# State-space outputs, decay gates and chunk products of neighbouring tiles in turn on groups of the array's columns and rows, with an arena of 64 slots

## The chip, the cores and the metric

One core of a Trainium2 chip runs the whole program. The metric is the device time of one execution in microseconds (us). Before the change three runs gave 1535.45, 1535.64 and 1537.04 us, the median 1535.64.

## What is computed

The reference passes 256 tokens of width 1024 through two blocks, in float32. The first block has two layers with attention, pooling and a gated linear attention (GLA). The second block has one layer: an RWKV recurrence and a state-space branch (S5) whose results are merged, and then a feed-forward part with a short convolution. Three places matter here.

The decay gates of the GLA, for both directions, from 16 columns each of the projected input:

```python
log_a_f = (jax.nn.log_sigmoid((zz['gla_af'] @ af_w2 + af_b).astype(f32)) / GLA_TAU)
log_a_b = (jax.nn.log_sigmoid((zz['gla_ab'] @ ab_w2 + ab_b).astype(f32)) / GLA_TAU)
```

The state-space branch: 32 groups of 64 complex states, run over the tokens, and read out by a complex matrix of which the real part counts:

```python
_, states = lax.associative_scan(s5_combine, (a_elems, bu), axis=1)
y = jnp.real(jnp.einsum('gcp,blgp->blgc', c, states)) + d * ug
y = jax.nn.gelu(y.reshape(bsz, L, S5_WIDTH))
```

The RWKV recurrence over the tokens, eight heads of 64, of which the kernel makes four chunks of 64 tokens:

```python
sa = jnp.einsum('bhij,bhj->bhi', S, a_t)
S = S * w_t[:, :, None, :] + sa[..., None] * b_t[:, :, None, :] + v_t[..., None] * k_t[:, :, None, :]
```

## The kernel before

All activations lie transposed, 128 features by 256 tokens (512 where context and sequence lie side by side). Weights come from one large array in units, by DMAs that SyncE (SP) issues (`unit`); `split` cuts each into a rounded high part `wh` (ScalarE, line 425) and a rest `wl` (VectorE or GpSimd, line 427), with four buffers of each, and `mm3` (line 442) multiplies with three products. Seven buffers hold raw weights.

Working tiles of 128x512 come from the `Arena`: NSLOT slots, a queue of free ones; `get` takes the oldest free slot and `put` hands one back at the end. Whoever writes a slot waits for its former readers. PSUM has four buffers for large products (`pmm`) and two each in the pools `pa` and `pb`.

The order of the work is made in two steps. The code of a branch is written as a generator, and `weave` runs two of them in turn by counts written by hand, a chain of dependent steps and a filler with independent products. The Tile framework then lays out each engine's instructions from that order, by priority and readiness, and sets the waits.

What the change touches:

`gla_decay` (line 1025), at the head of the GLA chain of each layer. For each of four heads it multiplies 32 rows (64 to 95) of the tile `misc` by 32 rows of `gw` into a PSUM tile `pgate` of 512 columns (line 1030), and VectorE adds a bias and makes the input of the logarithm (lines 1032 to 1034). Later, per level of the GLA, VectorE writes a fresh arena tile `E` at lines 1136 and 1137, out of two tiles that no matmul writes.

`s5_chain` (line 1543): sixteen tiles. For each, SP loads a table, PE makes `bu` (line 1587; two tiles at a time, in two groups of 32 rows), VectorE and GpSimd turn it (1590 to 1593), and a step later `recur` runs the recurrence on VectorE (scan at line 1559, products at 1560 and 1561, the last on GpSimd). Two steps later `output` (line 1564) makes the real output: four float32 products of 128 rows, 32 columns and 256 tokens, added up in one quarter (32 partitions) of a PSUM tile `py5`, which the traces call `py`. The quarter is i % 4. After each fourth tile VectorE (1575) and ScalarE take the sum. `py` is also the name of the attention's output (line 886), where products for two heads go in turn to two groups of 64 columns, and `pmod` (line 609) is filled by four products in turn in four groups of 32 columns.

```python
for n, (w_, x_) in enumerate(((cre, t1[:, 0:256]), (cren, t1[:, 256:512]), (cimn, t2[:, 0:256]),
                              (cimn, t2[:, 256:512]))):
    nc.tensor.matmul(pys[-1][rows, C], w_[:, cc_], x_, start=n == 0, stop=n == 3)
```

`rwkv_chain` (line 1643): products of 64 rows by 64 columns, each in one quarter of the array, which its operands' partitions and its output's partitions choose. Per head the scores `sc` (line 1771) and `scl` (1773), with `cp` (token half, output rows) outside and source inside; VectorE masks `sc` at 1776. Then inverses by doubling (`pQ`, `pY`, `pX`, lines 1800 to 1808), `pw` (1827, eight heads of one half and then eight of the other), and the loop over four chunks: `prh` (1846, four products for even heads, VectorE's sum, four for odd heads), `pu` (1853), the new state `pmn` (1861, 1862, per head k and then b), the output `pyo` (1868, 1869, likewise) and `pyi` (1878). `bonus_of` (line 1682), `head_bcast` (`hb`, line 1668, from a copy at 1665) and `nk` (1657) belong to its preparation.

A float32 matmul of the program runs as two records in the trace, two passes with a weight load each.

The chain and the branch are woven by these lines at the end of `second_block`: the columns of the RWKV part with seven steps of the state-space chain, then fourteen steps of the RWKV chain with five, ten with the rest, and what is left with `merge1`.

Of the kernel before, what the change touches and what calls it, by code (L numbers as in the profile page):

```python
# [27 lines left out]
FF = 2816  # L28
MLA_SCALE = 96 ** -0.5
TAU = 16.0  # L30
NSLOT = 62
MOD_AT = (0, 1, 4)
S5_EARLY = (7, 5)


# [44 lines left out]
def _pad_rows(a, at, rows=P):  # L80
    out = np.zeros((rows, a.shape[1]), a.dtype)
    out[at:at + a.shape[0]] = a
    return out
# [88 lines left out]
def _win_cols(w, name, t):  # L172
    if name == "misc":
        kr = w[:, OFF["kr"]:OFF["kr"] + 32]
        z = np.zeros((D, 32), w.dtype)
        return np.concatenate([kr, kr[:, ROPE_PERM], w[:, OFF["af"]:OFF["af"] + 32], z], 1)
    o = OFF[name] + P * t
    return w[:, o:o + P]

# [111 lines left out]
def gate_weights(inp, l):  # L291

    gw = np.zeros((32, 4, 2, 64), np.float32)
    gw[:16, :, 0] = np.asarray(inp["gla_af_w2"][l]).reshape(16, 4, 64)
    gw[16:, :, 1] = np.asarray(inp["gla_ab_w2"][l]).reshape(16, 4, 64)
    return _pad_rows(gw.reshape(32, 512), 64)

# [375 lines left out]
def trunk(b, l, xs, st, A):  # L675
# [349 lines left out]

    def gla_decay():
        es = []
        for hd in range(4):
            ps = b.pa.tile([P, 512], F32, tag="p", name="pgate")
            nc.tensor.matmul(ps, gw[64:96, hd * P:(hd + 1) * P], misc[64:96], start=True, stop=True)  # L1030
            e, a = S.get(), S.get()
            nc.vector.tensor_scalar(a, ps, v("gb", hd), None, ALU.add)
            nc.vector.scalar_tensor_tensor(e, a, -1.0, a, ALU.mult, ALU.min)
            nc.vector.tensor_scalar(a, a, 0.0, None, ALU.min)
            nc.scalar.activation(e, e, AF.Exp)
            es.append(e)
            la.append(a)
        one = b.after(es, 1.0)
        for e in es:
            nc.scalar.activation(e, e, AF.Ln, bias=one)  # L1040
        for e, a in zip(es, la):
            nc.vector.tensor_sub(a, a, e)
            S.put(e)
        S.put(misc, gw)
# [423 lines left out]
def second_block(b, xs, st, A):  # L1468
# [74 lines left out]
    def s5_chain():  # L1543
# [17 lines left out]
            nc.gpsimd.tensor_tensor(h2(t2), h2(g5), h2(tab)[:, ::-1], ALU.mult)  # L1561
            S.put(g5, tab)

        def output(i):
            _, t1, t2 = parts[i]
            rows, cc_ = slice(32 * (i % 4), 32 * (i % 4) + 32), slice(32 * i, 32 * i + 32)
            if i % 4 == 0:
                pys.append(b.pb.tile([P, 512], F32, tag="p", name="py5"))
            for n, (w_, x_) in enumerate(((cre, t1[:, 0:256]), (cren, t1[:, 256:512]), (cimn, t2[:, 0:256]),
                                          (cimn, t2[:, 256:512]))):  # L1570
                nc.tensor.matmul(pys[-1][rows, C], w_[:, cc_], x_, start=n == 0, stop=n == 3)
            S.put(t1, t2)
            if i % 4 == 3:
                u_ = us[i // 4]
                nc.vector.scalar_tensor_tensor(u_.ap, u_.ap, v("d", i // 4), pys[-1][:, C], ALU.mult, ALU.add)
                nc.scalar.activation(u_.ap, u_.ap, AF.Gelu_apprx_tanh)

        for i in range(16):
            tab = S.get()
            nc.sync.dma_start(tab, b.s5["tab"][i])  # L1580
# [13 lines left out]
            parts.append((tab, t1, t2))  # L1594
            if i:
                recur(i - 1)
            if i > 1:
                output(i - 2)
            yield
        recur(15)  # L1600
        output(14)
        output(15)
        S.put(*s5w, sbr, sbi)
        wg = b.unit(("glu",))
        ysp = []
# [35 lines left out]
    def rwkv_chain():  # L1641
# [116 lines left out]
        for bt in range(2):  # L1758
            Lm, Y, X_ = S.get(), S.get(), S.get()
            for hd in range(4 * bt, 4 * bt + 4):  # L1760
# [3 lines left out]
                pl_ = b.pa.tile([P, 512], F32, tag="p", name="scl")  # L1764
                ar3 = AR[q].rearrange("p (a t) -> p a t", a=2)
                for cc in range(2):
                    for cp in range(2):
                        t0 = cc * P + cp * CH
                        orow = slice(cp * CH, cp * CH + CH)
                        for n, src in enumerate((BT, KT)):  # L1770
                            nc.tensor.matmul(ps[orow, cc * 256 + n * P:cc * 256 + n * P + P].rearrange("p (a t) -> p a t", a=2),
                                             src[q].ap[rows, t0:t0 + CH], ar3[rows, :, t0:t0 + CH], start=True, stop=True)
                        nc.tensor.matmul(pl_[orow, cc * CH:cc * CH + CH], AR[q][rows, t0:t0 + CH], BT[q].ap[rows, t0:t0 + CH],
                                         start=True, stop=True)
                g = S.get()
# [43 lines left out]
        W = []  # L1819
        for cc in range(2):  # L1820
            ps = b.pb.tile([P, 512], F32, tag="p", name="pw")
            for cp in range(2):
                rr = slice(cp * CH, cp * CH + CH)
                for hd in range(8):
                    hc = slice(hd * 64, hd * 64 + 64)
                    g0 = cc * 256 + P
                    nc.tensor.matmul(ps[rr, hc], G[hd][rr, g0:g0 + CH], tok["v", cc][rr, hc], start=True, stop=True)
            t = S.get()
            nc.scalar.copy(t, ps)
            W.append(t)  # L1830
            yield
# [3 lines left out]
        for c in range(4):  # L1835
# [3 lines left out]
            rhs, U = W[cc], S.get()  # L1839
            w4 = rhs.rearrange("p (q e i) -> p q e i", e=2, i=64)  # L1840
            if c:
                for e in range(2):
                    rows = slice(64 * e, 64 * e + 64)
                    prh = b.pa.tile([P, 512], F32, tag="p", name="prh")
                    for q in range(4):
                        nc.tensor.matmul(prh[rr, q * 64:q * 64 + 64], AR[q][rows, t0:t0 + CH], M[rows, q * 64:q * 64 + 64],
                                         start=True, stop=True)
                    nc.vector.tensor_add(w4[rr, :, e], w4[rr, :, e], prh[rr, 0:256].rearrange("p (q i) -> p q i", i=64))
            pu = b.pb.tile([P, 512], F32, tag="p", name="pu")
            for hd in range(8):  # L1850
# [4 lines left out]

            if c < 3:
                pm = b.pa.tile([P, 512], F32, tag="p", name="pmn")
                for hd in range(8):
                    rows, hc = slice(64 * (hd % 2), 64 * (hd % 2) + 64), slice(hd * 64, hd * 64 + 64)
                    qc = slice(hd // 2 * 64, hd // 2 * 64 + 64)  # L1860
                    nc.tensor.matmul(pm[rows, qc], tok["k", cc][rr, hc], tok["v", cc][rr, hc], start=True, stop=False)
                    nc.tensor.matmul(pm[rows, qc], tok["b", cc][rr, hc], U[rr, hc], start=False, stop=True)
            pyo = b.pb.tile([P, 512], F32, tag="p", name="pyo")
            for hd in range(8):
                rows, hc = slice(64 * (hd % 2), 64 * (hd % 2) + 64), slice(hd * 64, hd * 64 + 64)
                qc = slice(hd // 2 * 64, hd // 2 * 64 + 64)
                g0 = cc * 256 + CH
                nc.tensor.matmul(pyo[rows, qc], tok["v", cc][rr, hc], G[hd][rr, g0 + P:g0 + P + CH], start=True, stop=False)
                nc.tensor.matmul(pyo[rows, qc], U[rr, hc], G[hd][rr, g0:g0 + CH], start=False, stop=True)
            yc = lambda q: ys[q].ap[:, t0:t0 + CH]  # L1870
            for q in range(4):
                nc.scalar.copy(yc(q), pyo[:, q * 64:q * 64 + 64])
# [248 lines left out]
```

## Time and profile before

| | before |
|---|---|
| median of three runs | 1535.64 us |
| the profiled execution, time | 1536.71 us |
| its span, first to last instruction | 1534.9 us |
| instructions | 27423 |
| mean granted clock of TensorE, share of full | 0.96 |
| TensorE busy | 1427.4 us |
| VectorE busy | 1070.7 us |
| ScalarE busy | 713.5 us |
| GpSimd busy | 433.8 us |
| DMA | 187.91 MB |

The rows further below come from that execution. PE is TensorE's matmul, PEld its weight load, which runs beside matmuls, DVE is VectorE, ACT ScalarE, POOL GpSimd. A busy share is an average over stages with different limits, and matmuls are pipelined: a record's duration has its run-out in it, so a burst's length is read from its start to the start of what follows. A view by stretch shows the limits of one stage, a view of waits names who was waited for, and a timeline shows bursts.

### The profile page before, as it was taken

To read this page: it belongs to the slowest core of one execution; us is meant where nothing else is said; L and a number is where in the kernel's file an instruction comes from. 1 tells how busy PE (TensorE), PEld (TensorE's weight loads), DVE (VectorE), ACT (ScalarE), POOL (GpSimd) and SP (SyncE) were. 2 spreads that over 40 slices of the span, in tenths; PEclk is the share of its full clock that TensorE was granted. 3 is DMA by queue.
4 is the path that set the end of the run, shared out by engine and by line. 5 is a ranking of instruction groups with operands and counts; after the bars stand their busy time and mean duration, and the time that the engine had idled before them with its cause. 6 is when DMAs were issued, how large, how long until landed. Compare 5 with 4: busy or idle time off the path is not lost. (4 is left out here: it accounts for less than half of the span.)

```text
span 1534.9 us, 27423 instructions
## 1 busy us (share of the span) xinstructions
PE 1427.4 (93%) x10700; PEld 1212.0 (79%) x10700; DVE 1070.7 (70%) x2113; ACT 713.5 (46%) x1307; POOL 433.8 (28%) x428
## 2 busy tenths in 40 slices
PE   5999999999899999899998899979899999799997
PEld 1676776777788788886877789978668999699997
DVE  4455557877779865755589876758988549698843
ACT  3434445343433764454454445633532435366642
POOL 1010003445341004520035341344644003521212
PEclk8999999999999999999989999978999999799999
DMA  9534440321133363335024335844221325266660
GB/s 358 185 109 141 134 149 17 104 76 56 45 94 117 130 197 99 97 110 165 19 79 124 91 111 172 266 141 125 78 84 37 98 62 169 74 206 181 179 187 32
DMA packets 61041, 187.91 MB, mean 122 GB/s; under 512 B 7024, under 2 KB 8560, under 8 KB 60912
## 3 DMA queue, kind: packets, MB, share of 16 engines
q1 hardware_dynamic: 60912, 186.17, 38.5%
q8 instruction: 84, 1.38, 0.4%
q14 instruction: 45, 0.37, 0.1%
HBM read 180.11 MB, written 6.03 MB: 121 GB/s over the span
## 5 line engine op out<-in xcount | busy, mean ns | idle before, releaser
L425 ACT CAST wh<-raw 128x1024 fp32r<-128x1024 f32 (+1 forms) x296 | 279.4, 949 | 255.9 <-PE y L442 50.6
L427 DVE TENSOR_TENSOR wl<-raw,wh 128x1024 fp32r<-128x1024 f32 (+1 forms) x225 | 263.1, 1170 | 163.9 <-ACT wh L425 160.9
L427 POOL TENSOR_TENSOR wl<-raw,wh 128x1024 fp32r<-128x1024 f32 (+1 forms) x71 | 144.6, 2037 | 641.9 <-ACT wh L425 624.8
L442 PE MATMUL z_merge<-s,wh 128*128 128x512 f32 (+1 forms) x768 | 199.6, 350 | 0.0
L442 PEld LDWEIGHTS z_merge<-s,wh 128*128 128x128 f32 x768 | 135.5, 197 | 17.4 <-issue 1.5
L442 PE MATMUL z_merge<-s,wl 128*128 128x512 f32 (+1 forms) x384 | 133.0, 346 | 0.0
L442 PE MATMUL pbr<-s,wh 128*128 128x256 f32 (+1 forms) x512 | 120.6, 327 | 2.9 <-ACT s L432 2.0
L442 PE MATMUL pup<-s,wh 128*128 128x256 f32 x656 | 118.5, 283 | 0.1
L442 PEld LDWEIGHTS pup<-s,wh 128*128 128x128 f32 x656 | 102.5, 192 | 0.2 <-ACT wh L425 0.2
L442 PE MATMUL y<-s,wh 128*128 128x256 f32 x496 | 99.6, 297 | 0.0
L442 PEld LDWEIGHTS pbr<-s,wh 128*128 128x128 f32 x512 | 86.8, 192 | 12.3 <-ACT s L432 2.6
L442 PE MATMUL pwo<-s,wh 128*128 128x256 f32 (+1 forms) x448 | 91.4, 302 | 2.3 <-ACT s L1251 1.7
L442 PE MATMUL pup<-s,wl 128*128 128x256 f32 x328 | 92.8, 283 | 0.0
L442 PEld LDWEIGHTS y<-s,wh 128*128 128x128 f32 x496 | 79.8, 196 | 7.4 <-issue 4.9
L442 PE MATMUL pbr<-s,wl 128*128 128x256 f32 (+1 forms) x256 | 83.1, 325 | 0.0
L442 PEld LDWEIGHTS z_merge<-s,wl 128*128 128x128 f32 x384 | 75.9, 198 | 8.5 <-issue 0.8
L442 PEld LDWEIGHTS pwo<-s,wh 128*128 128x128 f32 x448 | 73.1, 194 | 5.5 <-ACT s L1251 1.9
L1138 ACT ACTIVATE s<-s 128x512 f32<-128x512 f32 (+1 forms) x64 | 33.3, 524 | 89.1 <-DVE s L1137 77.9
L442 PE MATMUL y<-s,wl 128*128 128x256 f32 x248 | 71.7, 289 | 0.0
L432 ACT CAST s<-s 128x256 fp32r<-128x256 f32 (+1 forms) x88 | 42.6, 487 | 57.1 <-DVE s L1208 14.3
L442 PE MATMUL pwo<-s,wl 128*128 128x256 f32 (+1 forms) x224 | 67.6, 302 | 1.5 <-DVE wl L427 1.5
L442 PE MATMUL pdn<-s,wh 128*128 128x256 f32 x352 | 63.4, 283 | 0.0
(490 smaller groups left out, 3545.7 us busy)
## 6 DMA issues: line engine op xcount, KB each, us to landing
raw<-wts SPq DMA_DIRECT2D x294, 512.0 KB, 4.3
s<-wts SPq DMA_DIRECT2D x57, 256.0 KB, 5.1
s5t<-s SPq DMA_DIRECT2D x16, 256.0 KB, 2.0
s<-s5t SPq DMA_DIRECT2D x16, 256.0 KB, 3.3
s<-xc SPq DMA_DIRECT2D x8, 256.0 KB, 5.3
x<-xc SPq DMA_DIRECT2D x8, 256.0 KB, 5.0
s<-tabs SPq DMA_DIRECT2D x4, 256.0 KB, 3.8
out<-s SPq DMA_DIRECT2D x8, 128.0 KB, 1.8
```

The lines of the kernel that those rows point to most:

```text
L425: self.nc.scalar.copy(hi[:, :n], src)
L427: self.last_lo = eng.tensor_sub(lo[:, :n], src, hi[:, :n])
L432: self.nc.scalar.copy(hi, src)
L442: self.nc.tensor.matmul(ps, u, v[:, cols], start=start and n == 0, stop=stop and n == last)
L1138: nc.scalar.activation(E[:, lo:], E[:, lo:], AF.Exp, scale=1.0 / TAU)
```

## The change

Four sets of products get another order of issue, so that neighbours in the order lie in different groups of columns or of rows of the array. No product is added or dropped, and the operands and sums of each are as before.

- State-space outputs: `output` takes a group of tiles, `S5_GROUPS` (four, four, and four times two), and issues each of the four products for all tiles of the group before the next. A group is put out at the step at which its last tile was before; the tiles before it are held until then, and so are their slots.
- Decay gates: a second copy of the 32 gate columns stands in rows 96 to 127 of `misc` and of `gw` (zeros before), and heads go in pairs, the second on the copy, with both PSUM tiles of `pa` taken first.
- Chunk products: in `sc` the source is outside and `cp` inside; in `pw` the heads are outside and `cp` inside; `prh` has both tiles at once, with even and odd heads in turn; in `pmn` and `pyo` k, v or b go for two heads in turn.
- The arena has 64 slots in place of 62.

```diff
-NSLOT = 62
+NSLOT = 64
+S5_GROUPS = ((4, 0), (4, 4), (2, 8), (2, 10), (2, 12), (2, 14))
...
-        z = np.zeros((D, 32), w.dtype)
-        return np.concatenate([kr, kr[:, ROPE_PERM], w[:, OFF["af"]:OFF["af"] + 32], z], 1)
+        af = w[:, OFF["af"]:OFF["af"] + 32]
+        return np.concatenate([kr, kr[:, ROPE_PERM], af, af], 1)
...
-    return _pad_rows(gw.reshape(32, 512), 64)
+    gw = gw.reshape(32, 512)
+    return _pad_rows(np.concatenate([gw, gw]), 64)
...
+        pgs = []
         for hd in range(4):
-            ps = b.pa.tile([P, 512], F32, tag="p", name="pgate")
-            nc.tensor.matmul(ps, gw[64:96, hd * P:(hd + 1) * P], misc[64:96], start=True, stop=True)
+            if hd % 2 == 0:
+
+                pgs = [b.pa.tile([P, 512], F32, tag="p", name="pgate") for _ in range(2)]
+                for i, ps in enumerate(pgs):
+                    rr = slice(64 + 32 * i, 96 + 32 * i)
+                    nc.tensor.matmul(ps, gw[rr, (hd + i) * P:(hd + i + 1) * P], misc[rr], start=True, stop=True)
+            ps = pgs[hd % 2]
...
-        def output(i):
-            _, t1, t2 = parts[i]
-            rows, cc_ = slice(32 * (i % 4), 32 * (i % 4) + 32), slice(32 * i, 32 * i + 32)
-            if i % 4 == 0:
+        def output(group):
+
+            if group[0] % 4 == 0:
                 pys.append(b.pb.tile([P, 512], F32, tag="p", name="py5"))
-            for n, (w_, x_) in enumerate(((cre, t1[:, 0:256]), (cren, t1[:, 256:512]), (cimn, t2[:, 0:256]),
-                                          (cimn, t2[:, 256:512]))):
-                nc.tensor.matmul(pys[-1][rows, C], w_[:, cc_], x_, start=n == 0, stop=n == 3)
-            S.put(t1, t2)
+            for n, (w_, k, e) in enumerate(((cre, 1, 0), (cren, 1, 1), (cimn, 2, 0), (cimn, 2, 1))):
+                for i in group:
+                    rows, cc_ = slice(32 * (i % 4), 32 * (i % 4) + 32), slice(32 * i, 32 * i + 32)
+                    nc.tensor.matmul(pys[-1][rows, C], w_[:, cc_], parts[i][k][:, 256 * e:256 * e + 256],
+                                     start=n == 0, stop=n == 3)
+            for i in group:
+                S.put(*parts[i][1:])
+            i = group[-1]
...
-            if i > 1:
-                output(i - 2)
+            if i - 2 == groups[0][-1]:
+                output(groups.popleft())
...
-        output(14)
-        output(15)
+        for g in groups:
+            output(g)
...
                 for cc in range(2):
+                    for n, src in enumerate((BT, KT)):
+                        for cp in range(2):
+                            t0 = cc * P + cp * CH
+                            orow = slice(cp * CH, cp * CH + CH)
+                            nc.tensor.matmul(ps[orow, cc * 256 + n * P:cc * 256 + n * P + P].rearrange("p (a t) -> p a t", a=2),
+                                             src[q].ap[rows, t0:t0 + CH], ar3[rows, :, t0:t0 + CH], start=True, stop=True)
                     for cp in range(2):
...
-            for cp in range(2):
-                rr = slice(cp * CH, cp * CH + CH)
-                for hd in range(8):
+            for hd in range(8):
+                for cp in range(2):
+                    rr = slice(cp * CH, cp * CH + CH)
...
-                for e in range(2):
-                    rows = slice(64 * e, 64 * e + 64)
-                    prh = b.pa.tile([P, 512], F32, tag="p", name="prh")
-                    for q in range(4):
+                prhs = [b.pa.tile([P, 512], F32, tag="p", name="prh") for _ in range(2)]
+                for q in range(4):
+                    for e, prh in enumerate(prhs):
+                        rows = slice(64 * e, 64 * e + 64)
...
+                for q in range(4):
+                    for n, (nm, x_) in enumerate((("k", tok["v", cc]), ("b", U))):
+                        for hd in (2 * q, 2 * q + 1):
...
+            for q in range(4):
+                for n, (x_, o) in enumerate(((tok["v", cc], g0 + P), (U, g0))):
+                    for hd in (2 * q, 2 * q + 1):
```

## Rows read from the trace of the kernel before

**Rows 1.** The profile page, busy time of each engine over the span.
```profile
PE 1427.4 (93%) x10700; PEld 1212.0 (79%) x10700; DVE 1070.7 (70%) x2113; ACT 713.5 (46%) x1307; POOL 433.8 (28%) x428
```

**Rows 2.** Busy time by stretch: length, each engine, granted clock, DMA share, GB/s.
```profile
1049.50:1086.00 36.50, 36.50 (x229) 30.00 (x229) 29.89 (x56) 14.36 (x27) 15.54 (x15) 0.86 0.36 112
1086.00:1131.00 45.00, 37.69 (x280) 27.69 (x281) 43.62 (x63) 23.84 (x44) 28.48 (x24) 0.92 0.28 81
1131.00:1150.00 19.00, 18.84 (x167) 12.17 (x162) 14.24 (x25) 2.55 (x7) 4.92 (x5) 0.91 0.27 88
...
1150.00:1196.00 46.00, 45.78 (x869) 38.54 (x868) 37.83 (x59) 10.19 (x20) 15.73 (x14) 1.00 0.13 36
1196.00:1262.00 66.00, 65.79 (x927) 60.85 (x925) 31.66 (x82) 26.30 (x58) 5.28 (x4) 1.00 0.28 86
```

**Rows 3.** Waits of PE from 1086 to 1131: us, times, longest.
```profile
PE hb L1668 <- DVE s L1665: 4.9, 1, 4.9
PE sc L1771 <- DVE s L1776: 2.4, 1, 2.4
```

**Rows 4.** Waits of VectorE from 1049.5 to 1086.
```profile
DVE wl L427 <- ACT wh L425: 1.8, 2, 1.0
...
DVE m L1673 <- PE nk L1657: 1.4, 1, 1.4
```

**Rows 5.** Waits of VectorE from 1131 to 1150.
```profile
DVE s L1776 <- PE sc L1771: 3.3, 2, 2.0
```

**Rows 6.** Waits of VectorE from 1150 to 1196.
```profile
DVE wl L427 <- ACT wh L425: 3.8, 2, 2.9
DVE s L1796 <- PE py L1571: 1.7, 1, 1.7
```

**Rows 7.** Timeline of PE, state-space outputs: start, us to the last end, line, shape, count.
```profile
1049.59 2.90 PE L1571 MATMUL py<-s,s 128*32 128x256 f32 x8
...
1102.34 1.91 PE L1571 MATMUL py<-s,s 128*32 128x256 f32 x8
1104.19 0.39 PE L442 MATMUL y<-s,wh 128*128 128x256 f32 x1
...
1132.13 3.51 PE L1571 MATMUL py<-s,s 128*32 128x256 f32 x8 [0.16 <-DVE s L1776]
...
1193.66 2.81 PE L1571 MATMUL py<-s,s 128*32 128x256 f32 x16
```

**Rows 8.** Timeline of PE, products that already alternate between groups of columns or rows.
```profile
113.87 1.06 PE L609 MATMUL pmod<-raw,sc 128*32 128x512 f32 x8
...
169.88 1.08 PE L886 MATMUL py<-s,s 128*64 128x256 f32 x8
...
1109.51 1.13 PE L1587 MATMUL bu<-s,s 32*128 32x256 f32 x8
```

**Rows 9.** Timeline of PE, chunk products of the second block.
```profile
1210.00 1.85 PE L1827 MATMUL pw<-s,s 64*64 64x64 f32 x32
...
1225.09 0.33 PE L1868 MATMUL pyo<-s,s 64*64 64x64 f32 x4
1225.21 0.33 PE L1869 MATMUL pyo<-s,s 64*64 64x64 f32 x4
...
1229.91 0.96 PE L1846 MATMUL prh<-s,s 64*64 64x64 f32 x16
```

**Rows 10.** Timeline of PE, decay gates of the first layer.
```profile
240.99 1.12 PE L1030 MATMUL pgate<-s,s 32*128 32x512 f32 x2
...
243.04 1.98 PE L1030 MATMUL pgate<-s,s 32*128 32x512 f32 x4
...
246.10 1.12 PE L1030 MATMUL pgate<-s,s 32*128 32x512 f32 x2
```

**Rows 11.** Timeline of PE, the first wait after the decay gates, second layer.
```profile
790.69 0.43 PE L1089 MATMUL pst<-cons,s 128*128 128x128 f32 x2 [2.51 <-DVE s L1072]
```

**Rows 12.** Waits of VectorE from 250 to 420, lines that write a fresh slot.
```profile
DVE s L1136 <- PE ppool L994: 3.4, 2, 2.1
...
DVE s L1136 <- PE po L1163: 1.8, 1, 1.8
```

More of the change, by code (lines that the diff above doesn't have):

```diff
@@ L1576, in output @@
                 nc.scalar.activation(u_.ap, u_.ap, AF.Gelu_apprx_tanh)
+        groups = deque(range(o, o + n) for n, o in S5_GROUPS)
         for i in range(16):
@@ L1769, in rwkv_chain @@
                         orow = slice(cp * CH, cp * CH + CH)
-                        for n, src in enumerate((BT, KT)):
-                            nc.tensor.matmul(ps[orow, cc * 256 + n * P:cc * 256 + n * P + P].rearrange("p (a t) -> p a t", a=2),
-                                             src[q].ap[rows, t0:t0 + CH], ar3[rows, :, t0:t0 + CH], start=True, stop=True)
                         nc.tensor.matmul(pl_[orow, cc * CH:cc * CH + CH], AR[q][rows, t0:t0 + CH], BT[q].ap[rows, t0:t0 + CH],
@@ L1841, in rwkv_chain @@
             if c:
-                for e in range(2):
-                    rows = slice(64 * e, 64 * e + 64)
-                    prh = b.pa.tile([P, 512], F32, tag="p", name="prh")
-                    for q in range(4):
+                prhs = [b.pa.tile([P, 512], F32, tag="p", name="prh") for _ in range(2)]
+                for q in range(4):
+                    for e, prh in enumerate(prhs):
+                        rows = slice(64 * e, 64 * e + 64)
                         nc.tensor.matmul(prh[rr, q * 64:q * 64 + 64], AR[q][rows, t0:t0 + CH], M[rows, q * 64:q * 64 + 64],
                                          start=True, stop=True)
+                for e, prh in enumerate(prhs):
                     nc.vector.tensor_add(w4[rr, :, e], w4[rr, :, e], prh[rr, 0:256].rearrange("p (q i) -> p q i", i=64))
@@ L1857, in rwkv_chain @@
                 pm = b.pa.tile([P, 512], F32, tag="p", name="pmn")
[L1858 to L1862, printed above, removed]
-            pyo = b.pb.tile([P, 512], F32, tag="p", name="pyo")
[L1864 to L1869, printed above, removed]
+                for q in range(4):
+                    for n, (nm, x_) in enumerate((("k", tok["v", cc]), ("b", U))):
+                        for hd in (2 * q, 2 * q + 1):
+                            rows, hc = slice(64 * (hd % 2), 64 * (hd % 2) + 64), slice(hd * 64, hd * 64 + 64)
+                            nc.tensor.matmul(pm[rows, q * 64:q * 64 + 64], tok[nm, cc][rr, hc], x_[rr, hc],
+                                             start=n == 0, stop=n == 1)
+            pyo = b.pb.tile([P, 512], F32, tag="p", name="pyo")
+            g0 = cc * 256 + CH
+            for q in range(4):
+                for n, (x_, o) in enumerate(((tok["v", cc], g0 + P), (U, g0))):
+                    for hd in (2 * q, 2 * q + 1):
+                        rows, hc = slice(64 * (hd % 2), 64 * (hd % 2) + 64), slice(hd * 64, hd * 64 + 64)
+                        nc.tensor.matmul(pyo[rows, q * 64:q * 64 + 64], x_[rr, hc], G[hd][rr, o:o + CH],
+                                         start=n == 0, stop=n == 1)
             yc = lambda q: ys[q].ap[:, t0:t0 + CH]
```

## The prediction

> **What bounds the kernel now.** I read the profile page first: TensorE (PE) is busy for 93% of the span, VectorE (DVE) for 70% [rows 1]. Both are averages, so the next view is the table of busy time by stretch, over the part of the second block in which the state-space outputs and the chunk products lie [rows 2]. From 1049.5 to 1086 PE has no idle time and DVE 6.6 us (36.50 less 29.89). From 1086 to 1131 it is the other way round: DVE is idle for 1.4 us of 45, PE for 7.3, and the waits of PE name DVE both times, 4.9 and 2.4 us [rows 3]. So in this stretch DVE sets the pace. From 1131 to 1150 DVE has 4.8 us idle and PE almost none, from 1150 to 1196 DVE 8.2 us and PE 0.2, and from 1196 to 1262 PE is full and DVE half empty [rows 2]. The waits of DVE say whose lateness its idle time is: of the first stretch 1.8 us go to weight casts (whose buffers PE frees) and 1.4 to nk [rows 4]; of the third 3.3 us to the score products sc [rows 5]; of the fourth 3.8 to weight casts and 1.7 to py itself [rows 6]. PE bounds all stretches but one.
>
> **State-space outputs (the tiles are called py, line 1571).** Now each of the 16 tiles is a burst of eight records: four float32 products, each run as two passes, all into one group of 32 columns, hence one after the other. From one burst to the next instruction it is 1.85 us (1102.34 to 1104.19), so 0.22 us per record and 0.1 to change over [rows 7]. The trace has cases of what the change wants. Eight records of 128x32 with 512 columns, in four column groups in turn, take 1.06 us; at two times 0.22 us each they would need some 3.6 one after the other. Eight of 128x64 with 256 columns, two groups in turn, take 1.08 us instead of 1.91 [rows 8]. So a group of four tiles should last as long as one tile does now, about 1.87 us, and so should a group of two.
> The Trainium skill (TensorE: Matmul & The Clock Gate, Part 3: Packing small matmuls) has a rule against this: a weight load overlaps a matmul in flight only where the row group differs, and these tiles all share their 128 rows. By it the outputs would gain nothing; the trace disagrees, with the 1.06 us just told.
> PE time removed: three bursts of each group of four, 2 x 3 x 1.85 = 11.1; one burst of each of the pairs 8, 10 and 12, 5.55; of the last pair, which already runs as sixteen records in 2.81 us and so half side by side, 0.9. That is 17.5 us. Two of the bursts removed ran longer, 2.90 and 3.51 us instead of 1.91 [rows 7], in the stretches whose granted clock is 0.86 and 0.91 [rows 2]: 2.6 more. In all 20.1 us of PE.
> How much of it reaches the end is set by DVE, whose work does not change. Per stretch the gain is at most what PE saves, and at most DVE's idle time that PE causes:
> - 1049.5 to 1086 (tiles 0, 1, 2 leave): PE saves 2.84 + 1.85 + 1.85 = 6.5; DVE has 6.6 idle, of which some waits are not on PE. I take 5.
> - 1086 to 1131 (tiles 4, 5, 6 leave): PE saves 5.5, DVE has 1.4 left. I take 0.5; the rest turns into longer waits of PE behind hb and sc, which is what is late next.
> - 1131 to 1150 (tiles 8, 10): PE saves 3.45 + 1.85 = 5.3, DVE has 4.8. I take 4.
> - 1150 to 1196 (tile 12, and half of the last pair): PE saves 2.75, all of it below DVE's 8.2. I take 2.75.
> That is 12.2 us. Nothing is later for those who wait: the last tile of each group of four is put out at the step at which it was (steps 5, 9, 13 and the end), so DVE's line 1575 gets its sum no later, and the recurrence before it on DVE and GpSimd is untouched. From below: only the last stretch counts, 2.75. From above: 20.1.
>
> **Chunk products of neighbours.** The two pw bursts have 32 records in 1.85 us, sixteen on one quarter of the array and then sixteen on another; prh has 16 in 0.96 [rows 9]. In turn they should go at the rate of pyo, which has four records per 0.12 us already [rows 9], that is 0.03 each: pw saves (1.85 - 0.22) / 2 = 0.8 twice, prh (0.96 - 0.22) / 2 = 0.37 in each of three chunks. 2.7 us, in the stretch where PE is full. For pyo and pmn the new order asks for what the trace shows already: PE there runs ahead into the neighbour over the two records in between. sc has two products, so four records, per neighbour; I cost pyo, pmn and sc at nothing. Bounds for this part: 0, if the chain's copies on ScalarE lose their cover, and 3.5.
>
> **Decay gates.** Four products per layer of 32x512 go now one after the other: two records in 1.12 us, four in 1.98, two more in 1.12 [rows 10]. Two row groups side by side are shown by bu: eight records of 32x256 in 1.13 us [rows 8]. So two pairs of 1.12 take the place of 4.2; 2.0 us of PE per layer go, 4.0 in both. But after the first gate the reader is DVE, which has three passes over each gate's 512 columns; and what PE then does first is wait for the chain behind the gates, 2.51 us in the second layer for DVE line 1072 [rows 11]. A PE that arrives sooner waits longer. I take 0.5 of 4.0; bounds 0 and 4.0. The second half of misc and gw costs nothing: both were zero-filled to their full size already, and no transfer grows.
>
> **Arena of 64 slots.** Outputs held longer keep up to six more slots in the first half and two in the second; two are added, so the tightest place in the state-space stage stays about as tight. SP's loads of the tables (sixteen) take slots from the same queue and stand ahead of weight loads; the weights have seven buffers as cover, and without it a load held for one burst costs 1.9 us each. Elsewhere every slot comes back two takes later. Today DVE waits with line 1136, which writes a fresh slot, for PE's ppool 3.4 us and for po 1.8 [rows 12]; it reads nothing of either, so these are waits for the old reader of the slot. They may go, or others may come. I take 1.5, bounds -3.4 and 5.2.
>
> **Sum.** 12.2 + 2.7 + 0.5 + 1.5 = 16.9 us. The profiled execution took 1536.7 us beside a span of 1534.9; 1536.7 - 16.9 = 1519.8. The median shown is 1535.6, some 1.1 lower, so 1518.7, rounded to 1519.
>
> **The rivals.**
> - All of it arrives. If DVE's stretch to 1131 loosens too (several of its passes are far longer than their like, and the clock no longer falls), the gain is 20.1 + 3.5 + 2 + 3, 28.6 us: 1507 (each rival's time is taken from the median). For it: two bursts at the low clock go. Against it: 1.4 us of idle DVE in 45. Chance 0.14.
> - DVE keeps nearly all. If the whole of 1049.5 to 1150 is a DVE chain and only the part behind 1150 gains, it is 2.75 + 2.7, with slots and gates at nothing: 5.5 us, 1530. For it: DVE is at 97% from 1086. Against it: its waits on PE before and after. Chance 0.15.
> - Column groups do not run side by side here: each weight load waits for the matmul in flight on the same rows, or the framework's order of issue puts other matmuls between the products of a group. Then only chunk products and slots remain: some 4 us, 1532. (The first of the two is the rule of the Trainium skill told above, from TensorE: Matmul & The Clock Gate, Part 3.) The rows with 1.06 and 1.08 us speak against it. Chance 0.04.
> - Slower: the clock. PE's waits at hb and sc, 7.3 us together [rows 3], grow by what PE saves and DVE does not, by 1.5 us at the first and 5 at the second, to some 14. This stretch and those beside it are where the granted clock is already 0.92, 0.86 and 0.91 [rows 2]. PE's work from 1086 to 1131 is 37.7 us [rows 2], 5.5 of it gone: 32. If PE ran all of that at the lower of its two levels, it would need up to 64 us where the stretch now takes 45, 19 more. Less the 16.4 us gained elsewhere, and with a burst of the next stretch at 3.51 us again in place of 1.91, that is 4 us over: 1540. It decides from about 29 us of work at the lower level on. For it: the burst after the wait for sc took 3.51 us. Against it: the work in there is denser than before, not thinner. Chance 0.06.
>
> **How the numbers follow.** The forecast, with some of each stretch's DVE idle time won, has 0.61. 1519 is its time. With the first rival and the second the range must reach from 1507 to 1531; this holds 0.88 of the chance less the tails of the forecast, some 0.82. A measurement of this kernel can tell about 0.2%, 3 us, from no change. Faster by that needs less than 1532.5: forecast and first rival, nearly all of the second and part of the third, 0.87; within it 0.07; slower 0.06.
>
> **What would show it.** py should have six groups in place of sixteen bursts: 32 records in about 2 us twice, sixteen in about 2 three times and 2 at the end, where 2.81 stands. If a group of four lasts over 5 us, the column groups do not overlap. In the table by stretch PE's busy time should fall most before 1196 while DVE's stays; PE's wait behind hb or sc should grow above 4.9 and 2.4 us, and if it does not, DVE did not bound that stretch. The waits of DVE for weight casts and sc should shrink. pw should last about 1.05 us. The start of pw, 1210 now, should come some 13 us sooner, and if it comes 20 sooner the first rival is right. pgate should be two pairs of about 1.1 us, and PE's wait of 2.51 longer. A lower clock for more of 1049 to 1150, or new waits of line 1136, would make the forecast wrong.

## The result, and the profile after

The changed kernel took 1515.29 us (median of four runs, 1514.6 to 1521.18) beside 1536.34 for the kernel before in the same comparison: a ratio of 0.9861, with a 95% interval of 0.9835 to 0.9887. That is 21 us, where the forecast was 16.9 off its own baseline: 1519, range 1507 to 1531. The number is near, and the place of the gain is not where the forecast had put it: that it is near is luck, as the parts below show.

The profiled execution is the slowest of the four: 1521.18 us, span 1519.4; so the traces show 15.5 us of the 21. Busy time of each engine over the span, from its profile page, beside [rows 1]:

```profile
PE 1411.2 (93%) x10700; PEld 1212.4 (80%) x10700; DVE 1068.2 (70%) x2113; ACT 708.2 (47%) x1303; POOL 438.3 (29%) x428
```

TensorE (PE) lost 16 us of busy time; the shares have hardly moved. So the gain has to be looked up by stage. I cut five stretches out of both traces, between the same events: first decay gate to first product of the first layer's `pwo`; the second layer's decay gate to `pen`; the first `bu` to the first `pQ` (most of the state-space stage); `pQ` to `pw`; `pw` to `pmean` (the chunk products). Columns: window, length, busy time and count of PE, weight loads, VectorE, ScalarE, GpSimd, then the granted clock, DMA share, GB/s. Before:

```profile
240.99:573.09 332.10, 318.23 (x1849) 256.39 (x1848) 260.73 (x491) 158.36 (x245) 97.59 (x106) 0.98 0.30 95
768.72:1013.98 245.26, 217.10 (x1764) 204.08 (x1763) 192.27 (x397) 124.70 (x246) 95.09 (x115) 0.92 0.46 142
1031.34:1150.83 119.49, 111.17 (x818) 86.67 (x820) 104.64 (x162) 48.66 (x89) 60.38 (x52) 0.91 0.34 105
1150.83:1210.00 59.17, 58.74 (x1107) 50.41 (x1104) 47.42 (x77) 18.33 (x36) 17.14 (x15) 1.00 0.16 46
1210.00:1253.97 43.97, 43.97 (x629) 41.02 (x626) 16.94 (x48) 15.21 (x37) 2.58 (x2) 1.00 0.30 93
```

After:

```profile
238.81:563.48 324.67, 315.34 (x1853) 255.51 (x1852) 255.77 (x491) 153.85 (x241) 97.41 (x105) 0.98 0.32 99
761.94:1003.44 241.50, 215.49 (x1760) 203.40 (x1759) 192.06 (x397) 123.79 (x244) 95.43 (x114) 0.92 0.47 145
1020.18:1138.70 118.52, 101.40 (x797) 87.50 (x798) 108.05 (x162) 48.60 (x89) 62.70 (x52) 0.83 0.34 105
1138.70:1197.54 58.84, 58.06 (x1129) 50.83 (x1127) 48.45 (x78) 18.43 (x36) 17.03 (x15) 1.00 0.16 48
1197.54:1238.15 40.61, 40.52 (x628) 37.93 (x625) 16.36 (x47) 15.24 (x36) 2.60 (x2) 1.00 0.34 101
```

Line by line: 7.4 us shorter in the first layer's gated attention, 3.8 in the second's, 1.0 and 0.3 in the two parts of the state-space stage, 3.4 in the chunk products. Eleven of the 16 us stand in the first block, where the change has only the decay gates and the two slots. In the state-space stage PE was busy for 9.8 us less before `pQ`, and the stretch got 1.0 us shorter. The granted clock there fell from 0.91 to 0.83. Over both parts of the stage PE's busy time fell by 10.5 us, about half of the 20.1 that the forecast had.

The products themselves do what they should. Timeline of PE after (start, us to the last end, line, shape, count), the rows that answer to [rows 7, 9 and 10]:

```profile
238.81 1.12 PE L1037 MATMUL pgate<-s,s 32*128 32x512 f32 x2
240.87 1.13 PE L1037 MATMUL pgate<-s,s 32*128 32x512 f32 x4
243.05 1.12 PE L1037 MATMUL pgate<-s,s 32*128 32x512 f32 x2
...
1066.11 1.93 PE L1579 MATMUL py<-s,s 128*32 128x256 f32 x32
...
1134.96 3.09 PE L1579 MATMUL py<-s,s 128*32 128x256 f32 x16 [0.44 <-DVE s L1791]
...
1182.03 1.92 PE L1579 MATMUL py<-s,s 128*32 128x256 f32 x16
...
1197.54 1.10 PE L1842 MATMUL pw<-s,s 64*64 64x64 f32 x32
```

A group of four tiles takes 1.93 us where one tile took 1.91; `pw` 1.10 instead of 1.85. Column groups do overlap. The decay gates pair otherwise than forecast: head 0 alone, heads 1 and 2 side by side, head 3 alone.

And the longest waits of PE in the state-space stage, 1038 to 1138 (us, times, longest), beside 4.9 and 2.4 in [rows 3], the only two over 0.2 us before:

```profile
PE hb L1680 <- DVE s L1677: 7.6, 2, 4.6
PE ptk L1754 <- DVE s L1732: 3.2, 1, 3.2
PE sc L1783 <- DVE s L1586: 2.3, 1, 2.3
PE sc L1783 <- DVE s L1791: 1.1, 1, 1.1
```

PE now waits for VectorE at these three places for 14.2 us, and for 2.0 more at `bon`, `y` and `py`, where it waited for 7.5 us before: the time that the groups free turns into waiting.

### The profile page after: what moved, and what is told of

The parts are those of the page before. It is cut to its first block, busy times and chain, and to the rows that moved or that the text cites. A ratio compares the mean times of both kernels' runs of the same rounds, so it can differ in the third digit from the quotient of the medians.

```text
span 1519.4 us, 27398 instructions
## 1 busy us (share of the span) xinstructions
PE 1411.2 (93%) x10700; PEld 1212.4 (80%) x10700; DVE 1068.2 (70%) x2113; ACT 708.2 (47%) x1303; POOL 438.3 (29%) x428
## 3 DMA queue, kind: packets, MB, share of 16 engines
q8 instruction: 84, 1.38, 0.4%
## 5 line engine op out<-in xcount | busy, mean ns | idle before, releaser
L444 PE MATMUL y<-s,wh 128*128 128x256 f32 x496 | 104.2, 307 | 0.6 <-DVE s L1546 0.6
L444 PEld LDWEIGHTS y<-s,wh 128*128 128x128 f32 x496 | 84.6, 207 | 5.0 <-issue 2.1
L444 PE MATMUL y<-s,wl 128*128 128x256 f32 x248 | 75.1, 303 | 0.0
```

Source lines behind the costliest of these rows:

```text
L444: self.nc.tensor.matmul(ps, u, v[:, cols], start=start and n == 0, stop=stop and n == last)
```

## The experiments

Times of one comparison share their runs of the kernel before: 1538.36 us for the first four, 1536.62 for the next four, 1537.34 for the last four. Differences are told against these. Single runs scatter by some us whatever the kernel. The traces show one place of it: the stretch between the two layers (first `pwo` to the second gate) is 195.4 to 195.9 us long in the four traces with 62 slots and 195.6 to 199.2 in the ten with 64, with a mean granted clock of 0.97 at the short end and 0.95 at the long one. So a profile is compared by stage, and totals by medians.

**One part at a time.** The arena alone:

```diff
-NSLOT = 62
+NSLOT = 64
```

> The kernel before with 64 slots and nothing else. Theory A (the arena gives most: VectorE's line 1136 no longer waits for the old readers of its slot): 8 to 12 us faster than before, some 1526, nearly all of it before the second block starts, and the waits of line 1136 for ppool and po (5.2 us in the stretch from 250 to 420) gone. Theory B (the prediction's size: slots 1.5 us): 1533 to 1536, the second block starts at most 3 us earlier.

Measured: 1526.55, 0.9918 (0.9895 to 0.9941), 11.8 us faster. In its trace the first `bu` comes 10.8 us sooner, so nearly all of it stands before the second block, as theory A had it. The arena and the output groups:

```diff
-NSLOT = 62
+NSLOT = 64
+S5_GROUPS = ((4, 0), (4, 4), (2, 8), (2, 10), (2, 12), (2, 14))
... (`output` as in the change)
-            if i > 1:
-                output(i - 2)
+            if i - 2 == groups[0][-1]:
+                output(groups.popleft())
```

> 64 slots and the state-space outputs in groups. Theory A (VectorE and a lower clock eat the outputs' gain): at most 4 us faster than 64 slots alone, with the granted clock between the first bu and pw below 0.94. Theory B (the prediction's size: 12 us): 11 to 13 us faster than 64 slots alone.

Measured: 1527.03, 0.992 (0.9894 to 0.9947), 11.3 us faster: on top of the slots the groups bring nothing that can be told (their interval overlaps the other's nearly wholly). The decay gates alone:

```diff
-        return np.concatenate([kr, kr[:, ROPE_PERM], w[:, OFF["af"]:OFF["af"] + 32], z], 1)
...
+        return np.concatenate([kr, kr[:, ROPE_PERM], af, af], 1)
...
+            if hd % 2 == 0:
```

> The decay gates in pairs alone, 62 slots. Theory A (they share the first block's gain): 2 to 4 us faster than before. Theory B (the prediction: the next wait grows by what was saved): 0 to 1 us faster.

Measured: 1537.49, 0.999 (0.9973 to 1.0006): no difference. The chunk products alone (`sc`, `prh`, `pmn` and `pyo` likewise as in the change):

```diff
-            for cp in range(2):
-                rr = slice(cp * CH, cp * CH + CH)
-                for hd in range(8):
+            for hd in range(8):
+                for cp in range(2):
+                    rr = slice(cp * CH, cp * CH + CH)
```

> The chunk products' order alone, 62 slots. Both theories: 2.5 to 3.5 us faster than before, all of it between the start of pw and the first pmean (44.0 us before). A rival (the copies lose their cover): 0 to 1 us.

Measured: 1534.88, 0.9979 (0.9964 to 0.9995), 3.5 us faster; in its trace the stretch from `pw` to `pmean` is 3.4 us shorter, as in the changed kernel.

**What holds the state-space stage.** PE's saving there is real and does not arrive. Is it VectorE? Two kernels leave out VectorE's multiply behind the scan (16 of 1.2 us on average in the kernel with the arena alone), one with serial outputs and one with groups, both with 64 slots and no other part of the change:

```diff
-            nc.vector.tensor_mul(t1, g5, tab)
```

> 64 slots and the outputs one tile at a time as before; VectorE's multiplication by the table after the scan (line 1560, 16 times, 19 us) is left out. Theory A (VectorE paces the stage together with PE's 29 us of outputs): 2 to 8 us faster than 64 slots alone (1526.5). Theory B (PE paces it): within 2 us of it.

> The run before this one with the outputs in groups; the same multiplication is left out. Theory A (VectorE's pace hid the groups' gain): with VectorE relieved the groups are worth 5 to 12 us against the ungrouped version. Theory B (the lower granted clock or the column groups themselves take the gain, whatever VectorE does): 0 to 2 us.

Measured: 1524.36 (0.9923, 0.99 to 0.9945) with serial outputs, 1514.83 (0.9855, 0.9832 to 0.9878) with groups. The whole stage from the first `bu` to `pw`, in the four kernels that differ in these two things, by the same columns as above. Serial outputs, all of VectorE's work:

```profile
1020.54:1198.29 177.75, 168.47 (x1919) 134.85 (x1919) 155.80 (x239) 66.85 (x125) 76.77 (x67) 0.96 0.28 86
```

Groups, all of VectorE's work:

```profile
1014.12:1191.57 177.45, 161.46 (x1919) 140.76 (x1919) 155.28 (x239) 66.89 (x125) 78.96 (x67) 0.87 0.28 86
```

Serial outputs, without the multiply:

```profile
1013.66:1191.24 177.58, 169.63 (x1920) 136.65 (x1919) 139.17 (x223) 67.08 (x125) 75.00 (x67) 0.96 0.29 86
```

Groups, without the multiply:

```profile
1020.29:1188.25 167.96, 148.22 (x1920) 130.13 (x1920) 144.72 (x223) 66.95 (x125) 77.22 (x67) 0.95 0.30 91
```

This is the clearest reading of the study. Work taken from PE alone: 0.3 us. From VectorE alone: 0.2. From both: 9.8. Each is one trace, and the two traces of the changed kernel differ by 1.9 us over this stage, so the first two are nothing and the third is clear; the totals say the same, -0.5, 0.5 and 10.0 us beyond the arena's 11.8. Neither engine alone is the bound; with serial outputs both are nearly full (PE 169 of 178 us, VectorE 156), and easing one alone does not shorten the stage. Two things are in this at once: the multiply is VectorE's work and also a link between the scan and `py`, and the runs do not tell work and link apart. A column of the table speaks of the clock: with groups and a loaded VectorE it is 0.87, and 0.95 as soon as VectorE is eased. So in these traces the groups by themselves do not lower it; groups while PE waits for VectorE do. With VectorE eased the groups take 21.4 us off PE's busy time (169.63 to 148.22), about what the forecast had; with all of VectorE's work 7.0 (168.47 to 161.46). Whether the lower clock takes a part of the gain itself or only fills time that PE would wait anyway is not told apart here.

Next, more PE time in the changed kernel: each group's products issued twice.

```diff
-            for n, (w_, k, e) in enumerate(((cre, 1, 0), (cren, 1, 1), (cimn, 2, 0), (cimn, 2, 1))):
+            for n, (w_, k, e) in 2 * list(enumerate(((cre, 1, 0), (cren, 1, 1), (cimn, 2, 0), (cimn, 2, 1)))):
```

> The changed kernel with each group's products of the state-space outputs run twice, the second time over the first: 6 x 1.86 = 11.2 us more of PE work in that stage. Theory A (VectorE paces the stage, PE's time for the outputs is off the path): 0 to 3 us slower than the changed kernel, 1515 to 1518. Theory B (PE's time counts there): some 11 us slower, 1526.

Measured: 1531.78, 0.9964 (0.995 to 0.9978), 4.8 us under the kernel before where the changed kernel is 20 or 21 under: 15 to 16 us lost. One of its groups, and its stage:

```profile
1068.89 3.66 PE L1579 MATMUL py<-s,s 128*32 128x256 f32 x64
```

```profile
1022.62:1211.05 188.43, 170.21 (x2049) 143.98 (x2050) 153.97 (x238) 66.91 (x125) 77.46 (x67) 0.89 0.27 82
```

The stage is 11 us longer than after the change, for six groups that are each 1.7 us or more longer. So PE's idle time there is no slack. My reading is that a longer burst holds up the product behind it, VectorE waits for that, and PE later for VectorE: the two engines hand the work to and fro. Part of it goes through the arena: VectorE waits 3.4 us with its scan and 2.6 with line 1811 for `py`, where the changed kernel has 0.4 and 0.9; both write a fresh slot and read nothing of `py`, so they wait for an old reader that now takes longer.

The last of this set eases VectorE at GpSimd's cost: every second weight remainder (`wl`) on GpSimd in this stage, instead of every fourth.

```diff
+    b.lo_every = 2
...
+    b.lo_every = 4
```

> The changed kernel in which, from the state-space chain to its end, every second weight remainder goes to GpSimd in place of every fourth: some 6 of 20 fewer on VectorE at 1.16 us. Theory A: 2 to 6 us faster than the changed kernel, 1510 to 1513. Rival (GpSimd needs about 2 us for one and slows VectorE while it runs): the same or slower, 1515 to 1520.

Measured: 1526.57, 0.9937 (0.9916 to 0.9957): some 10 us slower than the changed kernel, and slower than either theory had it. The remainders on GpSimd, and the stage:

```profile
L429 POOL TENSOR_TENSOR wl<-raw,wh 128x1024 fp32r<-128x1024 f32 x10 | 27.5, 2745 | 6.4 <-ACT wh L427 6.4
```

```profile
1022.36:1207.26 184.90, 161.55 (x1920) 136.90 (x1920) 157.33 (x234) 67.26 (x125) 93.56 (x73) 0.89 0.28 83
```

One remainder takes 2.75 us on GpSimd where VectorE takes 1.4, and VectorE's busy time did not fall (157.3 with five remainders fewer, beside 156.5 and 155.1 in the two traces of the changed kernel): what it still does takes longer.

**The changed kernel, whole and less one part.** First once more as it is, with no edit:

> The changed kernel once more, on the chip of the three runs beside it, so that each part taken away or added is read from the same comparison. From the two runs of parts alone (arena -12, chunk products -3.5, decay gates -0.9, output groups about 0) a plain sum gives about 16 us under the kernel before; the first measurement of the changed kernel gave 21. If the parts simply add, 15 to 18 us under; if some of them are worth more together than alone, 19 to 23.

Measured: 1517.28, 0.9867 (0.9844 to 0.9889), 20.1 us faster. The parts alone sum to about 16, so some of them are worth more together. Without the groups, all else as changed:

```diff
-            if i - 2 == groups[0][-1]:
-                output(groups.popleft())
+            if i > 1:
+                output(i - 2)
```

> The changed kernel without the output groups alone (serial outputs of each tile, as before; 64 slots, decay gates and chunk products as changed). Theory 'VectorE bound': VectorE has 106 to 108 us of work in the 118 us from the first bu to the first pQ product, in either version, so the PE time that the groups free is waited away again: this run is within 3 us of the changed kernel. Theory 'groups worth something only together with the other parts': 5 us or more slower than the changed kernel. The prediction on record had 12.2 us for the groups.

Measured: 1519.86, 0.9882 (0.9864 to 0.9901), 17.5 us faster. The groups are worth 2.6 us by medians, within what the two intervals leave open. From the first `bu` to `pQ` and on to `pw`, without groups:

```profile
1017.32:1134.98 117.66, 109.19 (x818) 83.92 (x819) 106.30 (x162) 48.59 (x89) 60.42 (x52) 0.94 0.34 107
1134.98:1194.65 59.67, 58.73 (x1106) 50.37 (x1104) 49.53 (x78) 18.21 (x36) 16.40 (x15) 1.00 0.16 46
```

With them (the repeated changed kernel):

```profile
1021.75:1138.10 116.35, 99.90 (x798) 87.40 (x799) 106.08 (x161) 48.34 (x89) 62.55 (x52) 0.82 0.35 106
1138.10:1197.20 59.10, 58.08 (x1130) 50.82 (x1127) 49.01 (x79) 18.42 (x36) 17.00 (x15) 1.00 0.19 51
```

PE is busy for 9.3 us less before `pQ`, and the stage is 1.3 + 0.6 = 1.9 us shorter.

Then without the slots:

```diff
-NSLOT = 64
+NSLOT = 62
```

> The changed kernel with the arena of 62 slots instead of 64, all else as changed. Theory 'slots free the first block': 10 to 13 us slower than the changed kernel, nearly all of it before the first bu product, with the waits of line 1143 on ppool and po (VectorE) back in the trace. The prediction on record had 1.5 us for the slots; by that it would be 1 to 3 us slower.

Measured: 1536.27, 0.9996 (0.998 to 1.0012): 19.0 us slower than the changed kernel, and no longer faster than the kernel before. That is more than any theory on record had. By stage, its trace is 7.7 us longer than that of the repeated changed kernel in the first layer, 2.5 in the second and 6.6 in the state-space stage. Its first layer, and `pQ` to `pw`:

```profile
240.80:572.89 332.09, 317.61 (x1848) 255.98 (x1848) 260.86 (x491) 158.26 (x245) 97.65 (x106) 0.98 0.30 95
...
1143.61:1210.03 66.42, 61.78 (x1128) 53.60 (x1126) 48.01 (x78) 18.31 (x36) 18.75 (x15) 0.95 0.15 44
```

The first layer is as long as before the change (332.09 beside 332.10), though the new decay gates are in: there the gates are worth nothing, and the 7.4 us are all of the slots (with the arena alone it is 325.1). New is the second row: 66.4 us where the changed kernel takes 59.1. What waits there, from the timeline and from the waits of VectorE and PE:

```profile
1166.25 1.98 PE L1815 MATMUL pQ<-s,s 64*64 64x64 f32 x32 [2.63 <-DVE s L1811]
1168.27 1.27 DVE L1567 TENSOR_TENSOR_SCAN s<-s_rho,s 128x256 f32<-128x256 f32 x2 [2.16 <-PE pQ L1815]
```

```profile
DVE s L1811 <- POOL s L1569: 2.3, 2, 1.2
DVE s L1567 <- PE pQ L1815: 2.2, 1, 2.2
PE pQ L1815 <- DVE s L1811: 2.8, 2, 2.6
```

The scan of line 1567 writes a fresh slot and reads nothing of `pQ`; it waits for the slot's old reader. Line 1811 writes a fresh slot too, the operand of `pQ`, and waits for GpSimd's multiply of line 1569, of which it reads nothing; behind it PE stands idle for 2.6 us, and the clock from 1166 to 1180 is 0.76, with 1.98 us for a `pQ` of 32 records where 1.15 is usual. With 64 slots PE waits nowhere for line 1811. The three kernels with 62 slots and serial outputs take 59.1 to 59.2 us from `pQ` to `pw`. So 62 slots and groups together cost the 7.3 us: the groups hold two more slots for each tile kept back, and the next writer comes upon a slot that was given back only just before. This stretch was seen in one trace. SP's table loads do not show it: they wait 17.7 us there, and 19.6 in the repeated changed kernel.

What the slots do in the first block shows in the waits of VectorE where line 1136 (1143 or 1144 in the others) writes `E`: 3.4 and 1.8 us in [rows 12], beside 1.6 and 0.7 more in the same window that the prediction did not count:

```profile
DVE s L1136 <- POOL s L1143: 1.6, 1, 1.6
DVE s L1136 <- PE po L1161: 0.7, 1, 0.7
```

With 64 slots, in the kernel without groups, window 248 to 416:

```profile
DVE s L1143 <- POOL s L1150: 1.3, 1, 1.3
DVE s L1143 <- PE po L1168: 0.7, 1, 0.7
```

7.5 us became 2.0. GpSimd multiplies `E` (lines 1141 and 1143, later 1148 and 1150), and the product `plv` on PE needs that. PE's waits for these in the same two windows, before and without groups:

```profile
PE plv L1111 <- POOL s L1141: 5.5, 3, 3.2
PE plv L1111 <- POOL s L1143: 1.7, 1, 1.7
```

```profile
PE plv L1118 <- POOL s L1150: 0.9, 1, 0.9
```

So the late slot reached PE through `E`. Not all of it is gain: `plv`'s wait for ScalarE's line 1095 grew from 2.1 to 4.9, and all waits of PE in the window fell from 11.8 to 8.6 us. A second part of the gain stands further on. From 500 to 520 PE stood idle for 2.1 us and ran at a clock of 0.91 before; with the slots alone, 4.4 us earlier by then, the 20 us from about the same place on have PE full at 1.00, with 90 records instead of 71. PE waited there for ScalarE's line 432 (1.8 us); how the slots make that earlier was not followed.

```profile
500.00:520.00 20.00, 17.95 (x71) 14.17 (x70) 15.75 (x35) 12.28 (x16) 0.00 (x0) 0.91 0.38 122
```

```profile
495.00:515.00 20.00, 20.00 (x90) 16.57 (x89) 19.93 (x46) 9.81 (x14) 0.00 (x0) 1.00 0.31 97
```

**A version that follows from this.** If both engines must be eased, VectorE's small operations can go to ScalarE, which is busy 49 of 118 us there:

```diff
-        nc.vector.tensor_scalar(p[13].ap, p[13].ap, 0.5, 0.5, ALU.mult, ALU.add)
+        nc.scalar.activation(p[13].ap, p[13].ap, AF.Copy, bias=0.5, scale=0.5)
...
-            nc.vector.tensor_scalar(kk_.ap, p[4 + q].ap, v("kk", q), None, ALU.mult)
+            nc.scalar.mul(kk_.ap, p[4 + q].ap, v("kk", q))
...
-            nc.vector.tensor_copy(lt.ap.rearrange("p (a c) -> p a c", c=64), r[:, 4 * q:4 * q + 4].unsqueeze(2).broadcast_to((P, 4, 64)))
+            nc.scalar.copy(lt.ap.rearrange("p (a c) -> p a c", c=64), r[:, 4 * q:4 * q + 4].unsqueeze(2).broadcast_to((P, 4, 64)))
...
-            nc.vector.tensor_copy(pl, e1.ap.rearrange("p (c t) -> p c t", t=CH)[:, :, CH - 1])
+            nc.scalar.copy(pl, e1.ap.rearrange("p (c t) -> p c t", t=CH)[:, :, CH - 1])
```

> The changed kernel with 13 small VectorE operations of the RWKV stage moved to ScalarE (lines 1657, 1666, 1677, 1719: 2.5 + 1.5 + 1.0 + 2.5 = 7.5 us of VectorE's 108 in the stretch from the first bu to the first pQ product; ScalarE is busy 49 of 118 us there). The result is the same. Theory 'VectorE bound': that stretch was 118.5 us with VectorE at 91 percent; with 100.5 us of work at the same share it is 110 to 112, so 4 to 8 us faster than the changed kernel. Theory 'the half clock or the chain of products sets it': within 2 us of the changed kernel. If ScalarE's order makes the new work late, slower.

Measured: 1512.78, 0.9839 (0.9819 to 0.986): the lowest median of all, 4.5 us under the changed kernel of the same comparison, though the two intervals overlap. In its trace the stretch to `pQ` is 1.9 us shorter than in the repeated changed kernel and 4.1 shorter than in the first trace of it; 110 to 112 us were expected:

```profile
1014.32:1128.76 114.44, 97.15 (x796) 82.89 (x797) 103.79 (x149) 52.50 (x102) 63.30 (x52) 0.87 0.36 110
```

VectorE's busy time fell by 2.3 us only (106.1 to 103.8), not by 7.5. Its weight remainders grew instead: in the repeated changed kernel and in this one,

```profile
L429 DVE TENSOR_TENSOR wl<-raw,wh 128x1024 fp32r<-128x1024 f32 x14 | 19.5, 1391 | 4.0 <-ACT wh L427 4.0
```

```profile
L429 DVE TENSOR_TENSOR wl<-raw,wh 128x1024 fp32r<-128x1024 f32 x14 | 22.2, 1584 | 3.0 <-ACT wh L427 3.0
```

14 remainders cost 2.7 us more (2.1 against the first trace of the changed kernel), with GpSimd as busy as before beside them.

## Why the prediction was right and wrong

The time came out within 4 us by luck: two terms of the sum failed in opposite directions by about the same amount. Even a sign that the forecast had named came for another reason: `pw` starts 12.5 us sooner, some 13 as foretold, but 11.2 of them are there at the first `bu`, before the stage that was to give them.

**State-space outputs: 12.2 us forecast; 2.6 by medians and 1.9 in the traces in the changed kernel, nothing on top of the slots alone.** Right were the overlap of the column groups (1.93 us for four tiles), and that VectorE would hold what PE frees: PE's wait at `hb` grew to 7.6 us, `ptk` came with 3.2, `sc` grew only from 2.4 to 3.4, and VectorE's waits for weight casts and `sc` shrank from 3.3 us each to 1.0 and 0.2. The step that failed is how the rule "per stretch the gain is at most what PE saves, and at most DVE's idle time that PE causes" was used, and within it the 5 us for 1049.5 to 1086 and the 4 us for 1131 to 1150: each took most of a bound as gain. It took nearly all of VectorE's idle time [rows 2] as caused by PE's load, stretch by stretch, though 1.8 us of it stood at weight casts and 1.4 at `nk` [rows 4]. Nor did PE's saving of 20.1 us come whole: PE's busy time fell by 10.5, at the lower clock, and by 21.4 only where VectorE was eased. But what VectorE waits for in one stretch can be a product that PE makes late because PE waited for VectorE in the stretch before; that is my reading of the four kernels with and without the multiply: 0.3, 0.2, and 9.8 for both. The lower bound, 2.75, is about what came. The second rival had this mechanism, VectorE keeping nearly all, with a chance of 0.15; of its price the first half, 2.75 us, was right.

**Arena: 1.5 us forecast, 11.8 alone and 19.0 in the changed kernel measured.** The rows were read rightly as waits for a slot's old reader and then priced at a third, with 5.2 us as the upper bound. Three things failed. The bound took two rows of the first layer; line 1136 had 2.3 us more there and 1.1 in the second layer. It took a part of the wait as the price, where the delay went on to PE through `E`, and PE was idle at a lower clock later in the layer too. And "the tightest place in the state-space stage stays about as tight" was right, but its worth was not counted: without the two slots the stretch from `pQ` to `pw` is 7.3 us longer with groups, and the whole stage 182.0 us beside 178.7 before. The new waits of line 1136 that the forecast gave as a sign against itself did not come.

**Chunk products: 2.7 forecast, 3.4 measured.** Mechanism and place were right, in the stretch where PE is full. `pw` gave 0.75 twice and `prh` 0.9 of its 1.1; `pmn` and `pyo`, costed at nothing, gave 0.2 in a chunk (from the first `pmn` behind `pu` to the last `pyo` 1.85 us instead of 2.08 in the first chunk). `sc` lies outside this stretch, and with the chunk products alone the stretch that holds it is no shorter (119.65 beside 119.49).

**Decay gates: 0.5 forecast, 0.9 by medians with an interval that holds zero.** PE's gates became 0.9 us shorter in the first layer (5.4 us from the first start to the last end instead of 6.2) and 0.7 in the second, not 2, since heads 1 and 2 pair and 0 and 3 do not; that `pa` has only two buffers is my reading of it, not tried. In the first layer nothing of it arrives (332.09 beside 332.10; with the gates alone it is 336.3). PE's wait behind the gates in the second layer is as the forecast had it, little changed: 2.61 us beside 2.51 [rows 11]. The second layer is 242.44 and 242.59 us long in the two kernels with 62 slots and the gates, 244.75 and 245.26 in the two without: some 2.4 us that look like the gates. With 64 slots nothing of it is left: 238.2 to 240.4 without the gates, 239.2 to 241.5 with them.

**Rivals.** Column groups that do not overlap: no; four tiles that share all 128 rows take 1.93 us. The rule of the Trainium skill that was told there (TensorE: Matmul & The Clock Gate, Part 3: Packing small matmuls) does not hold for these products. The same section of the Trainium skill lists three column tiles side by side at 2.38 times the speed, with which the trace agrees; the prediction told the rule alone. Slower by the clock: its first half happened. PE's waits at the three places grew to 14.2 us (some 14 was forecast, at `hb` and `sc` alone, which have 11.0) and the clock fell to 0.83, yet the stage did not get longer. All of it arrives: no.

## What to carry to other kernels

Where two engines hand work to and fro and both are nine tenths full, idle time on either is not slack and not gain: price a saving on one engine near the lower bound unless the other is eased too (here 0.3 and 0.2 us alone, 9.8 together). A wait to write a buffer from whose old reader nothing is read is a shortage of buffers; add up every such row, over all layers; here the sum was 8.6 us, and the two slots brought 11.8 alone and 19.0 with the groups, so it was the lower end and not the upper. A change that holds buffers longer and a change that adds buffers have to be priced together.

## What was not expected of the hardware

The granted clock fell from 0.94 to 0.82 in the stretch to `pQ` when the groups made PE wait for VectorE at more places, by which part of PE's work ran at the lower of its two levels: the pair of tiles at 1134.96 took 3.09 us, at a mean clock of 0.61, where the one at 1182.03 took 1.92 at 1.00. Easing VectorE in other ways than by leaving work out gave back much less than the moved work: 7.5 us moved to ScalarE took 2.3 off its busy time, and remainders moved to GpSimd took nothing off, since VectorE's other operations became longer. The changed kernel's trace says this much of it: the multiply of line 1568 on VectorE takes 0.68 or 0.69 us nine times and 1.38 to 1.78 seven times, and all seven long ones began while GpSimd's multiply of line 1569 was running, which is so for three of the nine short ones, two of them within 0.05 us of its start or end. No run changed this alone.
